# A two-layer RWKV-7 / linear-attention / cross-attention trunk on one core: decay ahead of the attention heads, output gates ahead of the norm, a second query buffer, six early gates instead of four

## The chip, the cores and the metric

The kernel runs on one core of a Trainium2 chip, as one launch. The metric is the device time of that launch in microseconds, the median of several runs. TensorE (PE) does the matrix products, VectorE (DVE), ScalarE (ACT) and GpSimd (POOL) the elementwise work, and the queue of SyncE (SP) issues the DMAs. SBUF holds the working tiles, PSUM the results of products.

## The reference

Two layers, each on 512 tokens of 1024 channels (all float32):

```python
for l in range(DEPTH):                                   # DEPTH = 2
    x = x + 0.5 * swiglu_ffn(rmsnorm(x, ffn1_norm[l]), ffn1_w_in[l], ffn1_w_out[l])
    h = rmsnorm(x, mix_norm[l])
    u_rwkv, u_gla, u_xa, u_gate = split_cols(h @ w_in[l], ...)
    y_rwkv, v_first = rwkv7_mixer(u_rwkv, v_first, ...)  # 8 heads of 64, a recurrence over the tokens
    y_gla = gla_mixer(u_gla, ...)                        # 4 heads, chunks of 64, decay, RMS norm, SiLU gate
    y_xa = memory_attention(u_xa, rmsnorm(mem, mem_norm[l]), xa_w_kv[l])   # 4 heads, 256 memory rows
    gates = sigmoid(u_gate)                              # one per branch and channel
    merged = sum over the branches j of (branch_j @ w_branch[l, j]) * gates[j]
    x = x + merged @ w_out[l]
    x = x + 0.5 * swiglu_ffn(rmsnorm(x, ffn2_norm[l]), ffn2_w_in[l], ffn2_w_out[l])
return rmsnorm(x, final_norm)
```

In the linear attention (GLA) a pair of heads needs q, k and v (projections, a short causal convolution, SiLU), a decay E = exp(gcum) and F = exp(-gcum) from a projection `al`, masked products inside chunks, a recurrence over 8 chunks, and at the end `o * rsqrt(mean(o*o)) * norm_w * silu(go)`; `go` is the output gate.

## The kernel before

Everything is kept with channels on the partitions and the 512 tokens along the free axis. A large product is made of 128x128 weight blocks. Weights come from HBM as `wraw`; ACT copies them to a rounded part `whi`, DVE subtracts to get the rest `wlo` (L581 to L598), activations are split in the same way (`xhi` and `xlo`, `yh` and `yl`, `mhi` and `mlo`), and each block costs three matmuls (`mm3`, L608): hi times hi, hi times lo, lo times hi, all into one PSUM tile `ps_b` of 512 columns. There are three `ps_b` buffers. One projection of the normed input h (`proj`, L717) is 8 blocks, so 24 such matmuls; one product with a branch weight is 12. The text calls these matmuls large. The small ones are those of GLA, of the attention heads and of RWKV (`ps_i`, `ps_f`, `ps_c`, `ps_y`).

A layer is FFN1, the mixing stage (`mix`, L1271) and FFN2. The mixing stage computes the keys and values of the memory (`xa_proj`), the norm (`norm_mix`, L634), then the projection `al`, the attention heads 0 and 1, GLA pair 0, the shared parts of RWKV (`rwkv_lora`: six projections), GLA pair 1, and then RWKV in eight half steps (`rwkv_fill`, L1043). After each half step a share of a list of fillers is called: heads 2 and 3, and the gated outputs of GLA and of attention (`branch`, L1260: one gate projection of 24 large matmuls, one product of 12). The two projections that the next pair of RWKV heads needs (`rwkv_rkv`, L748) stand between these in the program. Last come four early gates for RWKV's own output (`gate`, L1254), RWKV's last output and the `w_out` product.

No order of instructions is written by hand. A recorder (class at L248) takes the program down as operations with dependencies, plans the order with a cost for each operation (`cost`, `run`, `plan`, L311 to L478), and issues it; each engine then works through its own order. On PE an operation of kind 0 (the small matmuls) goes before those of kind 1 (the large ones of `mm3`), and within a kind the program's order counts (L379). So the large matmuls run in the order of the program and are put wherever no small one is ready. A tile waits for the release of the tile `bufs` places ahead of it in the ring of its tag, so a large product waits until the `ps_b` three ahead of it has been read, and a large product that can't be read out holds up all large products behind it. A tile of a pool that opens waits until the pools closed before have been left by all their users (`Pool`, L193).

What the change and the prediction touch: `gla_pair` (L1165) calls `gla_conv` for q and k, then `gla_decay`; `gk` is the tile of k and then of each v, `gc` the scratch tile of the convolution and of the norm, each with one buffer; the gate projection `GGO` stands inside the norm at the pair's end, and SiLU of it is written to `gc2`. `xa_query` (L1091) puts a head's query into `xq`, which has one buffer, is overwritten with the head's result and is stored to `yx` by a DMA. `sumsq` and `rstd` (L646, L658) make the sum of squares `sqa` and the factor `rs` of a norm in the pool `nrm`, which stays open.

Of the kernel before, what the change touches and what calls it, by code (L numbers as in the profile page):

```python
# [11 lines left out]
F32 = mybir.dt.float32  # L12
# [7 lines left out]
P = 128  # L20
T = 512
# [473 lines left out]
class Net:  # L495
# [128 lines left out]

    def norm_in(self, name):
# [5 lines left out]
        rs, _ = self.rstd(self.x, T, D)  # L631
        return [(hi[:, k, :], lo[:, k, :]) for k in range(KD)], rs

    def norm_mix(self):  # L634
# [4 lines left out]
        rs, _ = self.rstd(self.x, T, D, copy=False)  # L639
# [6 lines left out]
    def sumsq(self, xs, n):  # L646
        nc = self.nc
        acc = self.nrm.tile([P, n], F32, name="sqa", tag="sqa")
        for k, x in enumerate(xs):
            if k == 0:  # L650
                nc.scalar.activation(acc, x, AF.Square)
                continue
            sq = self.nrm.tile([P, n], F32, name="sq", tag="sq", bufs=2)
            nc.scalar.activation(sq, x, AF.Square)
            nc.vector.tensor_tensor(acc, acc, sq, ALU.add)
        return acc

    def rstd(self, xs, n, dim, copy=True):  # L658
        nc = self.nc
        acc = self.sumsq(xs, n)  # L660
        nt = n // P
        ps = self.small()
        for t in range(nt):
            nc.tensor.matmul(ps[:, t:t + 1], acc[:, t * P:(t + 1) * P], self.c("ones")[:, 0:1], start=True, stop=True)
        rt = self.nrm.tile([P, nt], F32, name="rt", tag="rt", bufs=2)
        nc.scalar.activation(rt, ps[:, 0:nt], AF.Sqrt, bias=self.eps[:, 0:1], scale=1.0 / dim)
        nc.vector.reciprocal(rt, rt)
        ps = self.small()
        for t in range(nt):
            nc.tensor.matmul(ps[:, t * P:(t + 1) * P], rt[:, t:t + 1].to_broadcast([P, P]), self.c("ident"),  # L670
                             start=True, stop=True)
        if not copy:
# [135 lines left out]
    def rwkv_first(self, hp, hf, r, k, v, kk, kh, a, G):  # L808
# [85 lines left out]
        nc.vector.tensor_tensor(z4[:, :, 3:4], z4[:, :, 3:4], t4[:, :, 0:1], ALU.add)  # L894
        KH = rw.tile([P, 4, P], F32, name="KH", tag="KH", bufs=1)
        for c in range(4):
            nc.scalar.activation(KH[:, c, :], KBc[:, c, :], AF.Copy, scale=E[:, c, 64:65])

        ps = self.small("i")
        for c in range(4):  # L900
            nc.tensor.transpose(ps[:, c * P:(c + 1) * P], KH[:, c, :], self.c("ident"))
        KBT = rw.tile([P, 4, P], F32, name="KBT", tag="KBT", bufs=2)
# [188 lines left out]
    def xa_query(self, pool, j):  # L1091
        ps = self.proj(XQ + j)
        q = pool.tile([P, T], F32, name="xq", tag="xq", bufs=1)
        self.nc.scalar.activation(q, ps, AF.Copy)
        return q

    def xa_head(self, pool, j, q, kT, vm):
        nc = self.nc
        sc = 128.0 ** -0.5
        for hh in range(2):  # L1100
# [19 lines left out]
            pt = pool.tile([P, 2, 256], F32, name="pt", tag="pt", bufs=1)  # L1120
            nc.scalar.activation(pt, ps.rearrange("p (m t) -> p m t", m=2), AF.Copy)
# [42 lines left out]

    def gla_pair(self, pool, hp, al, yh, yl):  # L1165
        nc = self.nc
        t = lambda name, bufs=1: pool.tile([P, T], F32, name=name, tag=name, bufs=bufs)
        q, k = t("gq"), t("gk")
        self.gla_conv(pool, hp, q)
        self.gla_conv(pool, 2 + hp, k)  # L1170
        E, F = self.gla_decay(pool, hp, al)
        qz = self.qz
# [49 lines left out]
        for n in range(7):  # L1222
            src = kv[n % 2][:, (n // 2) * P:(n // 2 + 1) * P]
            if n == 0:
                nc.vector.tensor_copy(St[:, 0, :], src)
            else:
                nc.vector.scalar_tensor_tensor(St[:, n, :], St[:, n - 1, :], Ec[:, n, 63:64], src, ALU.mult, ALU.add)
        for j in range(2):
            h = 2 * hp + j
# [9 lines left out]
            nc.scalar.activation(o, ps, AF.Copy)  # L1239
            sq = t("gc")  # L1240
# [3 lines left out]
            sd = t("gc")  # L1244
# [26 lines left out]
    def mix(self):  # L1271
        nc, I, l = self.nc, self.I, self.l
        with ExitStack() as octx:
# [8 lines left out]
            kT, vm = self.xa_proj(self.keep, *ybuf())  # L1282
            self.h = self.norm_mix()

# [11 lines left out]
            with ExitStack() as ctx:  # L1296
# [6 lines left out]
                with ExitStack() as c2:  # L1303
# [31 lines left out]
            for m in range(KD):  # L1335
                self.branch(0, m, yh, yl, False, gates[m] if m < 4 else None)
                self.split(mhi[:, m, :], mlo[:, m, :], self.x[m], 0.5)
# [9 lines left out]
    def mem_norm(self):  # L1347

        nc, I = self.nc, self.I
        with ExitStack() as ctx:  # L1350
            pool = self.pool("memp", 1, ctx)
            mt = [pool.tile([P, NMEM], F32, name=f"m{k}", tag=f"m{k}") for k in range(KD)]
            for k in range(KD):
                nc.sync.dma_start(out=mt[k], in_=I["mem"][k * P:(k + 1) * P, :])
            rs, rt = self.rstd(mt, NMEM, D, copy=False)
            self.rsm = self.const.tile([P, NMEM], F32, name="rsm", tag="rsm")
# [4 lines left out]
    def finish(self, out):  # L1361
        nc = self.nc
        rs, _ = self.rstd(self.x, T, D, copy=False)
# [80 lines left out]
```

## Time and profile before

| | |
|---|---|
| median of 3 runs | 2858.64 us (2857.74 to 2858.75) |
| profiled execution | 2867.46 us |
| its span | 2865.7 us |
| mean granted TensorE clock | 0.976 |
| PE matmul busy | 2775.7 us (97%) |
| DVE, ACT busy | 1575.8 us (55%), 1167.4 us (41%) |
| DMA | 258.04 MB, mean 90 GB/s |

In the views below PE is the matmul engine and PEld the loading of its weights, which overlaps it. Matmuls are pipelined: one that starts every 0.227 us is shown with a length of 0.39 us, and so "busy" is the time in which at least one was under way. A bracket at the end of a row gives the idle time of that engine just before, and what ended it. PEclk is the share of the full TensorE clock that was granted. Tile names lose their buffer numbers. Nearly all instructions carry one line, L278, that of the recorder, so the reading goes by the tiles' names.

### The profile page before, as it was taken

Reading aid. Unit: us, or ns where it says so; the run is one execution under the profiler, and the core shown is the slowest. Engines: PE = TensorE matmul, PEld = TensorE weight load, DVE = VectorE, ACT = ScalarE, POOL = GpSimd, SP = SyncE. Lnnn points to the kernel's source line nnn. Section 1 sums busy time; section 2 is a strip of 40 time slices with the busy share of each in tenths; the row PEclk is TensorE's granted clock in tenths of the full one; section 3 lists DMA queues with packets and bytes.
Section 4 is the critical chain, followed back from the end, with each engine's and each line's share of the span. In section 5 each row is a group of like instructions: output and inputs, shape, how many; then the busy total and the mean of one; then the engine's idle time right before and its main releaser. Section 6 shows DMA issues by size and latency. Waiting matters only on the chain.

```text
span 2865.7 us, 35465 instructions
## 1 busy us (share of the span) xinstructions
PE 2775.7 (97%) x13280; PEld 2257.5 (79%) x13280; DVE 1575.8 (55%) x3056; ACT 1167.4 (41%) x2150; POOL 19.8 (1%) x102
## 2 busy tenths in 40 slices
PE   8999998998999899999999999989989998999998
PEld 6888887786788688888888888867777876888886
DVE  6434454675767655444554444655766685544443
ACT  5323345454445343323433233554544453432332
POOL 0000000000000000000000000000000000000000
PEclk9999997999999899999999999979999998999999
DMA  5232331211221132222322223312112211322222
GB/s 187 87 105 96 112 125 59 96 61 45 71 88 58 55 121 96 90 101 93 108 102 95 101 95 125 120 41 92 58 56 90 70 57 57 122 98 91 101 94 83
DMA packets 91723, 258.04 MB, mean 90 GB/s; under 512 B 10464, under 2 KB 24832, under 8 KB 91552
## 3 DMA queue, kind: packets, MB, share of 16 engines
q1 hardware_dynamic: 91552, 255.79, 25.8%
q8 instruction: 104, 1.70, 0.2%
q14 instruction: 67, 0.55, 0.1%
HBM read 243.69 MB, written 12.06 MB: 89 GB/s over the span
## 4 chain that ended last, share of the span: by engine, by line
PE 92%; DVE 5%; ACT 2%; issue 1%; DMA 1%; DVEq 0%; ACTq 0%; SPq 0%
PE ps_b L278 78%; PE ps_i L278 4%; PE ps_f L278 4%; PE ps_c L278 3%; PE ps_y L278 2%; DVE y L278 1%; DVE wlo L278 1%; ACT whi L278 0%; DMA x<-in_x_dram 0%; DVE Z L278 0%; ACT L278 0%; DVE st L278 0%; ACT VU L278 0%; DVE tt L278 0%; DVE t L278 0%
## 5 line engine op out<-in xcount | busy, mean ns | idle before, releaser
L278 ACT ACTIVATE whi<-wraw 128x512 fp32r<-128x512 f32 (+1 forms) x874 | 544.3, 623 | 1208.6 <-PE ps_b L278 1170.9
L278 PE MATMUL ps_b<-xhi,whi 128*128 128x512 f32 x2288 | 911.8, 399 | 16.3 <-ACT whi L278 9.7
L278 PE MATMUL ps_b<-xlo,whi 128*128 128x512 f32 x2288 | 906.7, 396 | 0.3 <-DVE xlo L278 0.3
L278 PE MATMUL ps_b<-xhi,wlo 128*128 128x512 f32 x2288 | 905.5, 396 | 1.1 <-DVE wlo L278 1.0
L278 DVE TENSOR_TENSOR wlo<-wraw,whi 128x512 fp32r<-128x512 f32 (+1 forms) x874 | 590.7, 677 | 573.9 <-ACT whi L278 572.4
L278 PEld LDWEIGHTS ps_b<-xhi,whi 128*128 128x128 f32 x2288 | 431.5, 189 | 112.0 <-ACT whi L278 11.6
L278 PEld LDWEIGHTS ps_b<-xhi,wlo 128*128 128x128 f32 x2288 | 430.9, 188 | 93.6 <-DVE wlo L278 3.9
L278 PEld LDWEIGHTS ps_b<-xlo,whi 128*128 128x128 f32 x2288 | 430.9, 188 | 92.9 <-issue 3.6
L278 PE MATMUL ps_b<-mhi,whi 128*128 128x512 f32 x704 | 277.4, 394 | 0.0
L278 PE MATMUL ps_b<-mhi,wlo 128*128 128x512 f32 x704 | 276.0, 392 | 0.0
L278 PE MATMUL ps_b<-mlo,whi 128*128 128x512 f32 x704 | 273.2, 388 | 0.0
L278 PEld LDWEIGHTS ps_b<-mhi,wlo 128*128 128x128 f32 x704 | 132.1, 188 | 31.0
L278 PEld LDWEIGHTS ps_b<-mlo,whi 128*128 128x128 f32 x704 | 132.2, 188 | 29.6
L278 PEld LDWEIGHTS ps_b<-mhi,whi 128*128 128x128 f32 x704 | 132.3, 188 | 26.3
L278 DVE TENSOR_TENSOR fm<-ps_b,ft 128x512 f32<-128x512 f32 x88 | 60.9, 692 | 127.7 <-PE ps_b L278 127.6
L278 DVE TENSOR_TENSOR ft<-ps_b,rs 128x512 f32<-128x512 f32 x88 | 60.9, 692 | 122.7 <-PE ps_b L278 122.5
L278 PE MATMUL ps_b<-yh,whi 128*128 128x512 f32 (+1 forms) x256 | 96.8, 381 | 4.6 <-ACT yh L278 4.6
L278 ACT ACT_TABLE_LOAD x73 | 93.7, 1283 | 17.6 <-DVE mx L278 7.7
L278 PE MATMUL ps_b<-yl,whi 128*128 128x512 f32 (+1 forms) x256 | 98.2, 384 | 0.0
L278 PE MATMUL ps_b<-yh,wlo 128*128 128x512 f32 (+1 forms) x256 | 97.1, 379 | 0.0
L278 DVE SCALAR_TENSOR_TENSOR x<-ps_b,x 128x512 f32<-128x512 f32 x64 | 44.3, 692 | 61.1 <-PE ps_b L278 61.0
L278 DVE TENSOR_TENSOR ft<-ft,rs 128x512 f32<-128x512 f32 x88 | 61.0, 693 | 13.5 <-ACT ft L278 5.4
(261 smaller groups left out, 2811.4 us busy)
## 6 DMA issues: line engine op xcount, KB each, us to landing
wraw<-in_ffn_in_dram SPq DMA_DIRECT2D x176, 512.0 KB, 3.4
wraw<-in_w_main_dram SPq DMA_DIRECT2D x108, 512.0 KB, 3.5
wraw<-in_ffn_out_dram SPq DMA_DIRECT2D x64, 512.0 KB, 3.5
wraw<-in_ffn_out_dram SPq DMA_DIRECT2D x64, 192.0 KB, 2.3
wraw<-in_w_branch_dram SPq DMA_DIRECT2D x48, 256.0 KB, 2.5
wraw<-in_w_out_dram SPq DMA_DIRECT2D x16, 512.0 KB, 3.4
xd<-x SPq DMA_DIRECT2D x16, 256.0 KB, 2.2
wraw<-in_w_k_dram SPq DMA_DIRECT2D x8, 512.0 KB, 3.6
```

The source lines that it names most:

```text
L278: return getattr(getattr(self.tc.nc, engine), what)(*(f(v) for v in a), **{n: f(v) for n, v in k.items()})
```

## The change

1. The decay of a GLA pair is computed first. `gla_pair` calls `gla_decay`, then a function `between` that it is given, then the convolutions of q and k. For pair 0 `between` is the attention heads 0 and 1, which stood ahead of the pair; for pair 1 it is `rwkv_lora`.
2. The two output gates of a pair (projection and SiLU) are computed ahead of the pair's norm loop, into the tile `gs` of the pool `mx`, instead of inside it into `gc2`.
3. `xq` gets two buffers, `gk` two, `gc` two (and `gc2` goes: the reciprocal is written in place). `pt` of a head takes the buffer of `pr`.
4. Head 3 stands after four outputs of GLA in the list of fillers, not after two.
5. Six early gates are made, not four; two new tiles `eg0` and `eg1` hold the added ones.
6. Space for this: `sqa` and `rs` of a norm are taken from the FFN's pool (or, in `mix`, from a pool `nm` that is open during `norm_mix` alone) instead of `nrm`; RWKV's tile `KH` goes, its values are written over `KB`.

```diff
-        acc = self.nrm.tile([P, n], F32, name="sqa", tag="sqa")
+        acc = pool.tile([P, n], F32, name="sqa", tag="sqa", bufs=1)
...
-        rs = self.nrm.tile([P, n], F32, name="rs", tag="rs", bufs=1)
+        rs = pool.tile([P, n], F32, name="rs", tag="rs", bufs=1)
...
             pool = self.pool("ffn", 2, ctx)
-            xs, rs = self.norm_in(norm)
+            xs, rs = self.norm_in(norm, pool)
...
-        KH = rw.tile([P, 4, P], F32, name="KH", tag="KH", bufs=1)
         for c in range(4):
-            nc.scalar.activation(KH[:, c, :], KBc[:, c, :], AF.Copy, scale=E[:, c, 64:65])
+            nc.scalar.activation(KBc[:, c, :], KBc[:, c, :], AF.Copy, scale=E[:, c, 64:65])
...
-        q = pool.tile([P, T], F32, name="xq", tag="xq", bufs=1)
+        q = pool.tile([P, T], F32, name="xq", tag="xq", bufs=2)
...
-        a = pool.tile([P, T], F32, name="gc", tag="gc", bufs=1)
+        a = pool.tile([P, T], F32, name="gc", tag="gc", bufs=2)
...
-    def gla_pair(self, pool, hp, al, yh, yl):
+    def gla_pair(self, pool, hp, al, yh, yl, between):
         nc = self.nc
         t = lambda name, bufs=1: pool.tile([P, T], F32, name=name, tag=name, bufs=bufs)
-        q, k = t("gq"), t("gk")
+        E, F = self.gla_decay(pool, hp, al)
+        between()
+        q, k = t("gq"), t("gk", 2)
         self.gla_conv(pool, hp, q)
         self.gla_conv(pool, 2 + hp, k)
-        E, F = self.gla_decay(pool, hp, al)
...
-            v = t("gk")
+            v = t("gk", 2)
...
+        gate = []
+        for j in range(2):
+            s = self.mx.tile([P, T], F32, name="gs", tag="gs", bufs=2)
+            nc.scalar.activation(s, self.proj(GGO + 2 * hp + j), AF.Silu)
+            gate.append(s)
         for j in range(2):
...
-            ri = t("gc2")
+            ri = sd
             nc.vector.reciprocal(ri, sd)
             nc.vector.scalar_tensor_tensor(o, o, self.pcol("gla_norm", h), ri, ALU.mult, ALU.mult)
-            s = t("gc2")
-            nc.scalar.activation(s, self.proj(GGO + h), AF.Silu)
-            nc.vector.tensor_tensor(o, o, s, ALU.mult)
+            nc.vector.tensor_tensor(o, o, gate[j], ALU.mult)
...
-            self.h = self.norm_mix()
+            with ExitStack() as ctx:
+                self.h = self.norm_mix(self.pool("nm", 1, ctx))
...
-                    head(0)
-                    head(1)
-                    self.gla_pair(gp, 0, al, yh, yl)
-                    self.rwkv_lora()
-                    self.gla_pair(gp, 1, al, yh, yl)
+                    self.gla_pair(gp, 0, al, yh, yl, lambda: (head(0), head(1)))
+                    self.gla_pair(gp, 1, al, yh, yl, self.rwkv_lora)
...
-                fill = [part(head, 2)] + [part(self.branch, 1, m, yh, yl, True) for m in range(2)] + [part(head, 3)]
-                fill += [part(self.branch, 1, m, yh, yl, True) for m in range(2, KD)]
+                fill = [part(head, 2)] + [part(self.branch, 1, m, yh, yl, True) for m in range(4)] + [part(head, 3)]
+                fill += [part(self.branch, 1, m, yh, yl, True) for m in range(4, KD)]
...
-                gates = [self.gate(0, m, eg[m // 2][:, (m % 2) * T:(m % 2 + 1) * T]) for m in range(4)]
+                eg = [e[:, i * T:(i + 1) * T] for e in eg for i in range(2)]
+                eg += [self.mx.tile([P, T], F32, name="early", tag=f"eg{i}", bufs=1) for i in range(2)]
+                gates = [self.gate(0, m, g) for m, g in enumerate(eg)]
```

The program has as many PE instructions as before and as many loads of ACT's tables (73); the planner puts them in another order. Three places on PE matter here.

The first is GLA pair 0, in layer 0. In the order before, these rows of PE stand where the keys of the pair are first transposed (`ps_i<-cst,gq`, then the first v, `gk`) and multiplied (`qz`, `kg`, `qr`, `kr`):

```order
L278 MATMUL ps_b<-xhi,whi 128x512
L278 MATMUL ps_b<-xlo,whi 128x512
L278 MATMUL ps_b<-xhi,wlo 128x512
L278 MATMUL ps_i<-cst,gq 128x128 x4
L278 MATMUL ps_i<-cst,gk 128x128 x4
L278 MATMUL ps_i<-qz_2887,kg 128x128
L278 MATMUL ps_i<-qr,kr 128x128
```

And of the change, at the same transposes:

```order
L278 MATMUL ps_b<-xhi,whi 128x512
L278 MATMUL ps_b<-xlo,whi 128x512
L278 MATMUL ps_i<-cst,gq 128x128 x4
L278 MATMUL ps_b<-xhi,wlo 128x512
L278 MATMUL ps_b<-xhi,whi 128x512
L278 MATMUL ps_b<-xlo,whi 128x512
L278 MATMUL ps_b<-xhi,wlo 128x512
L278 MATMUL ps_i<-qz_3021,kg 128x128
L278 MATMUL ps_i<-qr,kr 128x128
```

The transposes moved 70 rows up, and large matmuls now stand behind them. The product that the decay starts from (`ps_f<-al,aup`) stands 31 large matmuls ahead of these transposes before and 120 in the change.

The second place is where attention head 2 ends and head 3 begins (`kT,xq` are a head's scores, `pr` the transposes of its softmax, `pt,vm` its result; each twice in a head). Before, with the second half of head 2 and the first scores of head 3:

```order
L278 MATMUL ps_f<-cst,pr 128x128 x4
L278 MATMUL ps_f<-pt,vm 128x256 x2
L278 MATMUL ps_f<-kT,xq 128x256 x2
L278 MATMUL ps_f<-cst,pr 128x128 x4
L278 MATMUL ps_f<-pt,vm 128x256 x2
L278 MATMUL ps_f<-kT,xq 128x256 x2
L278 MATMUL ps_b<-xhi,whi 128x512
```

In the change, head 2 at its first softmax:

```order
L278 MATMUL ps_f<-cst,pr 128x128 x4
L278 MATMUL ps_b<-yh,wlo 128x512
L278 MATMUL ps_b<-xhi,whi 128x512
L278 MATMUL ps_b<-xlo,whi 128x512
L278 MATMUL ps_b<-xhi,wlo 128x512
L278 MATMUL ps_b<-xhi,whi 128x512
L278 MATMUL ps_f<-pt,vm 128x256 x2
L278 MATMUL ps_b<-xlo,whi 128x512
L278 MATMUL ps_b<-xhi,wlo 128x512
L278 MATMUL ps_b<-xhi,whi 128x512
L278 MATMUL ps_b<-xlo,whi 128x512
L278 MATMUL ps_f<-kT,xq 128x256 x2
```

Six groups of small matmuls stood behind one another with no large one between; now large ones of the gated outputs stand between all of them, and head 3 comes some 130 rows later.

The third place is the end of RWKV's recurrence in layer 0 (`ps_y<-S,AR`, `ps_f<-qs,Z` and `ps_f<-VU,KBT` are the steps of the chain, `ps_y<-VU,GR` its output, `ps_f<-cst,y` the transposes after the output's norm). Before:

```order
L278 MATMUL ps_f<-qs_85,Z 128x128
L278 MATMUL ps_f<-VU,KBT 128x128
L278 MATMUL ps_y<-S_89,AR 128x128
L278 MATMUL ps_f<-qs_91,Z 128x128
L278 MATMUL ps_y<-VU,GR 128x128 x4
L278 MATMUL ps_f<-cst,y 128x128 x2
L278 MATMUL ps_f<-sgl,g_221 128x256
L278 MATMUL ps_b<-yh,whi 128x512 x3
```

In the change:

```order
L278 MATMUL ps_f<-VU,KBT 128x128
L278 MATMUL ps_b<-xhi,whi 128x512
L278 MATMUL ps_b<-xlo,whi 128x512
L278 MATMUL ps_b<-xhi,wlo 128x512
L278 MATMUL ps_b<-yh,whi 128x512
L278 MATMUL ps_y<-S_89,AR 128x128
L278 MATMUL ps_b<-yl,whi 128x512
L278 MATMUL ps_b<-yh,wlo 128x512
L278 MATMUL ps_b<-yh,whi 128x512
L278 MATMUL ps_b<-yl,whi 128x512
L278 MATMUL ps_b<-yh,wlo 128x512
L278 MATMUL ps_f<-qs_91,Z 128x128
```

The last steps of the chain had no large matmul between them; now three to five stand between these, and 20 between `ps_y<-VU,GR` and `ps_f<-cst,y`. Behind `ps_f<-sgl,g` both orders read alike: large matmuls that need RWKV's last output.

More of the change, by code (lines that the diff above doesn't have):

```diff
@@ L623, in split, with norm_in @@
             nc.vector.scalar_tensor_tensor(lo, src, scale, hi.bitcast(F32), ALU.mult, ALU.subtract)
-    def norm_in(self, name):
+    def norm_in(self, name, pool):
         hi = self.keep.tile([P, KD, T], F32R, name="xhi", tag="xhi")
@@ L630, in norm_in, with norm_mix @@
             self.split(hi[:, k, :], lo[:, k, :], self.x[k], self.pcol(name, k))
-        rs, _ = self.rstd(self.x, T, D)
+        rs, _ = self.rstd(self.x, T, D, pool)
         return [(hi[:, k, :], lo[:, k, :]) for k in range(KD)], rs
-    def norm_mix(self):
+    def norm_mix(self, pool):
         nc = self.nc
@@ L638, in norm_mix @@
         lo = self.keep.tile([P, KD, T], F32R, name="xlo", tag="xlo")
-        rs, _ = self.rstd(self.x, T, D, copy=False)
+        rs, _ = self.rstd(self.x, T, D, pool, copy=False)
         for k in range(KD):
@@ L644, in norm_mix, with sumsq @@
         return [(hi[:, k, :], lo[:, k, :]) for k in range(KD)]
-    def sumsq(self, xs, n):
+    def sumsq(self, xs, n, pool):
         nc = self.nc
-        acc = self.nrm.tile([P, n], F32, name="sqa", tag="sqa")
+        acc = pool.tile([P, n], F32, name="sqa", tag="sqa", bufs=1)
         for k, x in enumerate(xs):
@@ L656, in sumsq, with rstd @@
         return acc
-    def rstd(self, xs, n, dim, copy=True):
+    def rstd(self, xs, n, dim, pool, copy=True):
         nc = self.nc
-        acc = self.sumsq(xs, n)
+        acc = self.sumsq(xs, n, pool)
         nt = n // P
@@ L894, in rwkv_first @@
         nc.vector.tensor_tensor(z4[:, :, 3:4], z4[:, :, 3:4], t4[:, :, 0:1], ALU.add)
[L895 removed]
         for c in range(4):
[L897 removed]
+            nc.scalar.activation(KBc[:, c, :], KBc[:, c, :], AF.Copy, scale=E[:, c, 64:65])
         ps = self.small("i")
         for c in range(4):
[L901 removed]
+            nc.tensor.transpose(ps[:, c * P:(c + 1) * P], KBc[:, c, :], self.c("ident"))
         KBT = rw.tile([P, 4, P], F32, name="KBT", tag="KBT", bufs=2)
@@ L1119, in xa_head @@
                     nc.tensor.transpose(ps[:, o:o + P], pr[:, t, m * P:(m + 1) * P], self.c("ident"))
-            pt = pool.tile([P, 2, 256], F32, name="pt", tag="pt", bufs=1)
+            pt = pool.tile([P, 2, 256], F32, name="pt", tag="pr", bufs=1)
             nc.scalar.activation(pt, ps.rearrange("p (m t) -> p m t", m=2), AF.Copy)
@@ L1239, in gla_pair @@
             nc.scalar.activation(o, ps, AF.Copy)
-            sq = t("gc")
+            sq = t("gc", 2)
             nc.scalar.activation(sq, o, AF.Square)
@@ L1335, in mix @@
             for m in range(KD):
-                self.branch(0, m, yh, yl, False, gates[m] if m < 4 else None)
+                self.branch(0, m, yh, yl, False, gates[m] if m < len(gates) else None)
                 self.split(mhi[:, m, :], mlo[:, m, :], self.x[m], 0.5)
@@ L1354, in mem_norm @@
                 nc.sync.dma_start(out=mt[k], in_=I["mem"][k * P:(k + 1) * P, :])
-            rs, rt = self.rstd(mt, NMEM, D, copy=False)
+            rs, rt = self.rstd(mt, NMEM, D, pool, copy=False)
             self.rsm = self.const.tile([P, NMEM], F32, name="rsm", tag="rsm")
@@ L1362, in finish @@
         nc = self.nc
-        rs, _ = self.rstd(self.x, T, D, copy=False)
+        rs, _ = self.rstd(self.x, T, D, self.nrm, copy=False)
         for k in range(KD):
```

2 lines of the change are left out of this document (1 added, 1 removed).

## The prediction

> **What bounds the kernel now.** I read the page first, then the idle time and the granted clock of PE stretch by stretch, then the rows that end the long waits. The page:
>
> ```profile
> span 2865.7 us, 35465 instructions
> PE 2775.7 (97%) x13280; PEld 2257.5 (79%) x13280; DVE 1575.8 (55%) x3056; ACT 1167.4 (41%) x2150; POOL 19.8 (1%) x102
> ```
>
> PE is busy in 97% of the span, so the number of matmuls bounds the kernel, and the change leaves that number alone. It can only touch the 90 us in which PE is idle, and the time that PE is busy at half its clock. Both sit in few places. The next view gives, for stretches that I cut at them, the length, then the busy time of PE (and the number of matmuls) and of the others; the third value from the right is PEclk, the granted clock.
>
> ```profile
> 30.00:376.00 346.00, 346.00 (x1524) 285.50 (x1523) 160.30 (x248) 117.11 (x190) 0.00 (x0) 1.00 0.30 104
> 460.50:466.80 6.30, 0.00 (x0) 0.00 (x0) 4.56 (x7) 4.82 (x6) 0.00 (x0) 0.75 0.20 73
> 466.80:494.80 28.00, 27.99 (x129) 23.05 (x130) 11.32 (x24) 8.70 (x13) 0.00 (x0) 0.51 0.00 1
> 494.80:515.00 20.20, 15.49 (x63) 11.18 (x62) 13.82 (x15) 16.03 (x22) 0.00 (x0) 1.00 0.15 54
> 655.00:685.50 30.50, 21.12 (x73) 14.71 (x72) 11.81 (x37) 9.90 (x26) 0.20 (x1) 0.78 0.07 22
> 685.50:957.00 271.50, 269.16 (x1544) 217.60 (x1542) 196.34 (x526) 129.44 (x307) 4.43 (x21) 1.00 0.21 70
> 957.00:985.80 28.80, 17.23 (x65) 12.51 (x65) 11.70 (x37) 6.63 (x18) 0.00 (x0) 0.70 0.05 17
> 1873.50:1879.80 6.30, 0.01 (x1) 0.01 (x1) 4.56 (x7) 4.82 (x6) 0.00 (x0) 0.75 0.19 74
> 1879.80:1908.00 28.20, 28.20 (x129) 23.26 (x129) 11.54 (x24) 8.69 (x12) 0.00 (x0) 0.50 0.00 1
> 1908.00:1930.00 22.00, 17.29 (x63) 11.92 (x62) 13.90 (x16) 16.32 (x22) 0.00 (x0) 0.94 0.16 57
> 2013.20:2016.70 3.50, 1.98 (x8) 0.69 (x6) 2.27 (x5) 3.09 (x4) 0.12 (x1) 0.99 0.39 145
> 2016.70:2020.10 3.40, 3.40 (x8) 2.72 (x9) 1.33 (x2) 1.25 (x2) 0.00 (x0) 0.50 0.01 5
> 2086.00:2105.40 19.40, 12.90 (x45) 9.32 (x44) 5.77 (x15) 6.87 (x19) 0.00 (x0) 0.74 0.04 14
> 2380.00:2409.00 29.00, 17.47 (x65) 12.96 (x66) 11.86 (x38) 6.63 (x18) 0.00 (x0) 0.71 0.02 8
> ```
>
> The first row is FFN1: no idle time, full clock, 346.00 / 1524 = 0.227 us for a large matmul; this is the price of filler. Then come three places per layer: GLA pair 0 (460 to 515, and 1873 to 1930), heads 2 and 3 inside RWKV (655 to 685, 2086 to 2105), the end of RWKV (957 to 985, 2380 to 2409). Between them, 685 to 957, PE is busy in 269.16 of 271.50 us. What ended the waits stands in brackets in the order of time:
>
> ```profile
> 466.81 1.12 PE L278 MATMUL ps_i<-cst,gq 128*128 128x128 f32 x4 [6.37 <-DVE gq L278]
> ...
> 679.08 0.60 ACT L278 ACTIVATE xq<-ps_b 128x512 f32<-128x512 f32 x1 [2.10 <-DMA yx<-xq]
> ...
> 679.73 2.07 PE L278 MATMUL ps_f<-kT,xq 128*128 128x256 f32 x4 [3.17 <-ACT xq L278]
> ...
> 977.43 0.66 PE L278 MATMUL ps_f<-cst,y 128*128 128x128 f32 x2 [5.77 <-DVE y L278]
> ...
> 981.25 1.22 PE L278 MATMUL ps_b<-yh,whi 128*128 128x512 f32 x2 [2.30 <-ACT yh L278]
> ```
>
> In each case the filler had run out. At 460 the gate projections of the pair hold two of the three `ps_b`, because their SiLU goes to a tile that the unfinished norm needs, and nothing large can start. At 677 head 3's query can't be written until head 2's result has left `xq` by DMA. At the end of RWKV the four early gates are used up, and three unfinished outputs, which need RWKV's last quarter, hold the three `ps_b`.
>
> **GLA pair 0.** The wait of 6.37 us is for the chain that begins with the decay:
>
> ```profile
> 453.21 0.69 ACT L278 ACTIVATE gz<-ps_f,par 128x512 f32<-128x512 f32 x1 [1.59 <-PE ps_f L278]
> ...
> 466.07 0.69 DVE L278 TENSOR_TENSOR gq<-kg,gE 128x512 f32<-128x512 f32 x1
> ```
>
> From `gz` to the end of `gq` it takes 13.6 us. Before, 31 large matmuls stand between the product that starts it and the transposes of `gq`: 31 x 0.227 = 7.0 us of cover. In the change there are 120, or 27 us, so the decay is no longer late. What is last there is then k's own convolution, with 29 large matmuls (6.6 us) and the small ones of head 1 behind k's product. I take the wait of 6.3 us in each layer as gone.
>
> The clock goes with it. After the wait the clock stays at 0.51 for 28.00 us though PE is busy in 27.99 of them. The same small matmuls in pair 1 at full clock give the price; first pair 0, then pair 1 (count, busy time, mean):
>
> ```profile
> L278 PE MATMUL ps_y<-qz,St 128*128 128x64 f32 x28 | 6.6, 373 | 0.0
> ```
>
> ```profile
> L278 PE MATMUL ps_y<-qz,St 128*128 128x64 f32 x28 | 4.3, 264 | 0.1
> ```
>
> By this ratio 28.0 us shrink by 28.0 x (1 - 4.3 / 6.6) = 9.8 us; if everything halves, by 14. I take 12 in layer 0, and 13 in layer 1, where the 22.00 us behind it ran at 0.94 (0.06 x 22 = 1.3).
>
> The Trainium skill, page "TensorE: Matmul & The Clock Gate", section "What's actually happening", says that one busy window of about 3.4 us brings the full clock back. The two rows at 466.80 and 1879.80 speak against it for small matmuls. By the rule a dip would be worth about 1.7 us, the two terms of 12 and 13 would shrink to that, and the total below would be an estimated 57 in place of 78, so 2802.
>
> The 4.7 us of idle time behind (20.20 - 15.49, 22.00 - 17.29) are waits for read-outs of `ps_b` behind the norm's reciprocals on DVE, with two buffers held by the gates. With SiLU of the gates ahead of the norm they are free; I take them as gone.
>
> What comes in place: the transposes of the second v. From the end of its product, its convolution runs through these steps (ACT scales, DVE adds three taps, with two masks `pf` of the products between, ACT's SiLU):
>
> ```profile
> 468.46 0.68 ACT L278 ACTIVATE gc<-ps_b,par 128x512 f32<-128x512 f32 x1
> ...
> 466.19 0.63 ACT L278 ACTIVATE gk<-gc 128x512 f32<-128x512 f32 x1 [1.40 <-DVE kr L278]
> ...
> 561.80 2.31 DVE L278 SCALAR_TENSOR_TENSOR gc<-ps_b,par,gc 128x511 f32<-128x511 f32 x3
> ...
> 554.84 0.75 DVE L278 TENSOR_TENSOR pf<-ps_i,cst 128x256 f32<-128x256 f32 x2
> ```
>
> 0.68 + 2.31 + 0.75 + 0.63 = 4.4 us, about 5.4 with the hand-overs. In the change's order PE has five large matmuls (1.1 us) and some twelve small ones (about 2) meanwhile, so 2.5 us stay open, and 1.5 more where the chunk recurrence `St` is built: 4 us of new waits, between 0 (the large matmuls of the first gate are ready and may have been placed well) and 7. Sum: 6.3 + 12 + 4.7 - 4 = 19 in layer 0, 20 in layer 1.
>
> **Heads 2 and 3.** Idle time: 30.50 - 21.12 = 9.4 us and 19.40 - 12.90 = 6.5. The two buffers remove the wait for the DMA, and with head 3 behind four outputs of GLA there are large matmuls between all small groups of head 2 (second place of the order). I leave 1.5 and 1 us idle. The clock: 0.22 x 30.5 = 6.7 us if PE were busy throughout the slow part, 6.7 - 9.4 / 2 = 2.0 if all idle time lay in it; I take 3.5, and 2.5 in layer 1 (5.0 and 1.8 by the same steps). Sum: 11.4 and 8. The projections of the next RWKV heads stand behind these fillers in the program, so the recurrence goes on earlier by the same time.
>
> **The end of RWKV.** Idle time: 28.80 - 17.23 = 11.6 us, 29.00 - 17.47 = 11.5. Two more gates are 48 x 0.227 = 10.9 us of filler, taken out of the stretch behind, where PE is the bound. They don't fit wholly: the last wait of 2.30 us has the same rows around it as before, and of the 5.77 us the 20 large matmuls now placed there cover 4.5, so 3.5 us stay idle and 8 go; the other 2.9 us of filler stretch the chain. The clock: 0.30 x 28.8 = 8.6 at most, 8.6 - 11.6 / 2 = 2.8 at least; 3 go, since the 3.5 us that stay idle may still cost a short dip. Sum: 11 in each layer.
>
> **What the space costs.** `sqa` in the FFN's pool waits for the pools before it to be left, so the sum of squares starts only after the last matmul of the stage before. In `mix` the norm's factor then reaches PE after 97 of the memory's 144 large matmuls, not after 37, and the norm's work falls on a DVE that is full:
>
> ```profile
> 383.00:401.00 18.00, 18.00 (x108) 15.86 (x107) 17.73 (x32) 11.90 (x21) 0.00 (x0) 1.00 0.42 146
> ```
>
> 24 of these 32 steps still lie behind the factor, 24 x 17.73 / 32 = 13.3 us, against 47 + 21 large matmuls (15.4 us) until `al` needs the last of them. That nearly fits; 1 us per layer, between 0 and 3. At the FFN starts the factor comes after 45 or 46 large matmuls (43 and 21 before), at the first one after 62 (40 before); it is needed when the fourth product wants a `ps_b`, after 72. Nothing there. `KH` over `KB`, `pt` over `pr`, the reciprocal in place: each waits for readers that are done first; nothing. Without that cover the cost would be a fraction of a microsecond in each of 16 half steps.
>
> **Sum.** 19 + 20 + 11.4 + 8 + 11 + 11 - 2 = 78.4 us. The profiled execution took 2867.46 us, 8.8 more than the median of 2858.64; 78.4 us from it is 2789.1, and from the median 2780.
>
> **Rivals.** (A) *The clock falls in the new GLA block all the same.* The rows at 2013.20 and 2016.70 show the price of short waits: 1.98 us busy of 3.50, and the next 3.4 us at 0.50. Two to four microseconds of waits among few large matmuls can do this, and the small ones behind stay slow until large ones follow, which in the change is soon (13 and 24 in a row after the pair). About half the old dip, 6 us a layer: 2780 + 12 = 2792; if it begins early, all 25: 2805. For it: this block has the fewest large matmuls. Against it: pair 1, ordered likewise, has no such dip. 35%. The Trainium skill, page "TensorE: Matmul & The Clock Gate", section "A second HAM failure mode: psum-queue depth-cycling", says that short idle times between groups of matmuls make the clock swing; the row at 2013.20 agrees.
>
> (B) *The fillers are given back.* If RWKV's chain and not PE limits 685 to 957, the gain at heads 2 and 3 (19.4 us) returns as idle time at RWKV's end: 2780 + 19.4 = 2799. Against it: 269.16 of 271.50 us busy. 12%.
>
> (C) *The norm's factor comes too late* (slower). Five norms now start after the last matmul of the stage before, and the first of all comes later too. If the factor came after more than 72 large matmuls, all three `ps_b` would stand full and PE would wait. To turn the sum it would have to cost over 13 us at each of six starts, that is to come 70 or more large matmuls later than it stands: 2865. 3%.
>
> (D) *The order is made for the planner's costs, and on the chip the added large matmuls stand in the way of the chain* as much as they fill: no change, 2859. 2%.
>
> **How the numbers follow.** My forecast, 2780, has 48%; its own bounds (new waits 0 to 7 us a layer, clock 9.8 to 14, heads' and end's clock, the norm) reach from 2762 to 2796. The range goes up to take in A and B: 2762 to 2808. A measurement of this kernel can tell about 0.2%, 6 us, from no change; beyond that faster has 0.95, within it 0.02, slower 0.03.
>
> **What would show it.** Right: no wait over 3 us before `ps_i<-cst,gq`, PEclk near 1.00 through GLA pair 0, no `xq` waiting for a DMA, the wait before `ps_f<-cst,y` at about 1.3 us and the one before `ps_b<-yh,whi` still 2.3. Wrong: PEclk at 0.5 for 10 us or more in GLA pair 0 (A), more idle time at RWKV's end than 4 us (B), waits of `ps_b` products for `rs` or `xlo` (C).

## The result, and the profile after

| | before | after |
|---|---|---|
| median | 2858.69 us (2857.74 to 2861.76, 4 runs) | 2769.98 us (2768.55 to 2770.58, 4 runs) |
| profiled execution, its span | 2867.46 us, 2865.7 us | 2769.8 us, 2768.0 us |
| mean granted TensorE clock | 0.976 | 0.995 |
| PE busy | 2775.7 us | 2731.8 us |
| span less PE busy | 90.0 us | 36.2 us |

The change makes the kernel 88.7 us faster, a ratio of 0.9687 (95% interval 0.967 to 0.9704). 2780 with a range of 2762 to 2808 was forecast.

The page of after:

```profile
span 2768.0 us, 35481 instructions
PE 2731.8 (99%) x13280; PEld 2225.2 (80%) x13280; DVE 1570.7 (57%) x3056; ACT 1164.9 (42%) x2150; POOL 19.8 (1%) x102
```

The same 13280 matmuls, 43.9 us less busy time on PE (the clock) and 53.8 us less idle time: 97.7 us between the two profiled executions. The view by stretches has the places of before again, in the same columns (length, busy time of PE, PEld, DVE, ACT and POOL, then PEclk; the last two are the DMA's busy share and its GB/s):

```profile
383.00:401.00 18.00, 18.00 (x96) 13.96 (x96) 15.63 (x28) 12.03 (x22) 0.28 (x6) 1.00 0.43 150
436.00:467.00 31.00, 30.85 (x196) 24.40 (x195) 19.97 (x41) 19.87 (x31) 0.00 (x0) 1.00 0.16 57
467.00:525.00 58.00, 57.78 (x254) 47.16 (x252) 36.19 (x49) 33.61 (x50) 0.20 (x2) 1.00 0.35 123
640.00:700.00 60.00, 59.34 (x356) 47.69 (x356) 46.37 (x128) 33.05 (x84) 0.93 (x5) 1.00 0.18 58
934.00:947.10 13.10, 9.24 (x30) 6.87 (x29) 7.18 (x22) 3.50 (x6) 0.00 (x0) 0.74 0.07 21
1806.00:1833.00 27.00, 26.85 (x179) 21.09 (x178) 17.42 (x38) 16.67 (x26) 0.00 (x0) 1.00 0.13 44
1833.00:1890.00 57.00, 57.00 (x238) 43.08 (x237) 31.48 (x41) 31.84 (x48) 0.20 (x2) 1.00 0.35 119
2000.00:2060.00 60.00, 58.76 (x324) 47.10 (x324) 45.81 (x130) 33.68 (x79) 1.13 (x6) 1.00 0.22 72
2311.50:2322.70 11.20, 7.69 (x24) 5.56 (x23) 6.21 (x19) 3.08 (x5) 0.00 (x0) 0.70 0.00 0
```

The first row is the memory's keys beside the norm (no idle time). The second and third are GLA pair 0 of layer 0 with the end of its norm, the sixth and seventh the same in layer 1: 0.37 us idle (0.15 + 0.22) and 0.15 us where 11.0 stood (6.3 + 4.7), at full clock. Heads 2 and 3 (fourth and eighth) have 0.7 and 1.2 us idle in 60, none of it before a head's matmuls. At the end of RWKV 3.9 and 3.5 us are left, in the waits that the forecast left there (timeline of PE, layer 0, then layer 1):

```profile
938.11 0.41 PE L278 MATMUL ps_f<-cst,y 128*128 128x128 f32 x2 [1.21 <-DVE y L278]
...
941.61 1.65 PE L278 MATMUL ps_b<-yh,whi 128*128 128x512 f32 x3 [2.65 <-ACT yh L278]
...
2314.24 0.41 PE L278 MATMUL ps_f<-cst,y 128*128 128x128 f32 x2 [1.20 <-DVE y L278]
...
2317.38 1.65 PE L278 MATMUL ps_b<-yh,whi 128*128 128x512 f32 x3 [2.30 <-ACT yh L278]
```

The one place of pair 0 where the forecast put new waits is the second v. Its product ends at about 447.9 us, its transposes stand last in these rows of PE:

```profile
447.75 1.03 PE L278 MATMUL ps_f<-pt,vm 128*128 128x256 f32 x4
448.71 0.49 PE L278 MATMUL ps_i<-qz,kg 64*128 64x128 f32 x2
...
450.40 0.48 PE L278 MATMUL ps_b<-xhi,whi 128*128 128x512 f32 x1
...
451.51 0.48 PE L278 MATMUL ps_i<-qz,kg 64*128 64x128 f32 x2
...
452.59 0.50 PE L278 MATMUL ps_b<-xlo,whi 128*128 128x512 f32 x1
452.93 0.60 PE L278 MATMUL ps_i<-cst,gk 128*128 128x128 f32 x4
```

No row has a bracket, and those left out have none either: PE waited nowhere in these 5.0 us.

### The profile page after: what moved, and what is told of

Its sections match the earlier page's. It is cut to its first block, busy times and chain, and to the rows that moved or that the text cites. A ratio compares the mean times of both kernels' runs of the same rounds, so it can differ in the third digit from the quotient of the medians.

```text
span 2768.0 us, 35481 instructions
## 1 busy us (share of the span) xinstructions
PE 2731.8 (99%) x13280; PEld 2225.2 (80%) x13280; DVE 1570.7 (57%) x3056; ACT 1164.9 (42%) x2150; POOL 19.8 (1%) x102
## 5 line engine op out<-in xcount | busy, mean ns | idle before, releaser
L278 PEld LDWEIGHTS ps_b<-mlo,whi 128*128 128x128 f32 x704 | 132.1, 188 | 29.6
L278 DVE TENSOR_TENSOR ft<-ft,rs 128x512 f32<-128x512 f32 x88 | 60.9, 693 | 14.1 <-ACT ft L278 6.3
```

Of the source, the lines that this page charges most:

```text
L278: return getattr(getattr(self.tc.nc, engine), what)(*(f(v) for v in a), **{n: f(v) for n, v in k.items()})
```

## The experiments

Twelve kernels. Eleven start from the changed kernel (2769.98 us) and one from the kernel before. The kernel before ran beside them at medians of 2860.4 (first four below), 2855.6 (next four) and 2857.5 us (last four).

| kernel | median us | ratio to before (95%) | against after |
|---|---|---|---|
| decay late | 2769.88 | 0.9685 (0.9666 to 0.9704) | -0.1 |
| gates late | 2771.97 | 0.9692 (0.9673 to 0.9711) | +2.0 |
| both late | 2799.61 | 0.9789 (0.9769 to 0.9808) | +29.6 |
| decay late, one gk | 2769.46 | 0.9683 (0.966 to 0.9705) | -0.5 |
| four early gates | 2793.30 | 0.9769 (0.9752 to 0.9785) | +23.3 |
| heads as before | 2792.26 | 0.9770 (0.9751 to 0.9789) | +22.3 |
| GLA pair as before | 2792.83 | 0.9767 (0.9745 to 0.9789) | +22.9 |
| eight early gates | 2756.72 | 0.9644 (0.9629 to 0.9659) | -13.3 |
| GLA pair as before, one xq | 2808.60 | 0.9827 (0.9809 to 0.9845) | +38.6 |
| one xq | 2773.01 | 0.9700 (0.9684 to 0.9715) | +3.0 |
| head 3 early | 2769.97 | 0.9689 (0.9674 to 0.9705) | 0.0 |
| space alone, on before | 2856.09 | 0.9995 (0.9986 to 1.0005) | |

**Decay late.**

```diff
-        E, F = self.gla_decay(pool, hp, al)
-        between()
         q, k = t("gq"), t("gk", 2)
         self.gla_conv(pool, hp, q)
         self.gla_conv(pool, 2 + hp, k)
+        E, F = self.gla_decay(pool, hp, al)
...
-                    self.gla_pair(gp, 0, al, yh, yl, lambda: (head(0), head(1)))
-                    self.gla_pair(gp, 1, al, yh, yl, self.rwkv_lora)
+                    head(0)
+                    head(1)
+                    self.gla_pair(gp, 0, al, yh, yl)
+                    self.rwkv_lora()
+                    self.gla_pair(gp, 1, al, yh, yl)
```

> The changed kernel with item 1 alone undone: the decay stands behind the convolutions of q and k again, heads 0 and 1 ahead of pair 0, the shared parts of RWKV ahead of pair 1. Gates ahead of the norm and second buffers stay. In the order about 65 large matmuls now stand between the decay's product and the transposes of gq (31 before, 120 in the change): 65 x 0.227 = 14.8 us against a chain of 13.6 us. Theory 1 (the wait is a matter of the large matmuls that can start, and the clock falls only after a wait): wait of 0 to 1.5 us, no dip, 2770 to 2776. Theory 2 (the decay's place is the cause, whatever the gates do): the wait of 6.3 us and the dip come back, 19 + 20 us less the 9.4 us of later waits, about 2800.

2769.88 us: nothing comes back. The stretch of its pair 0, at full clock with 0.8 us idle:

```profile
445.00:490.00 45.00, 44.20 (x247) 34.59 (x248) 29.94 (x49) 31.61 (x43) 0.05 (x1) 1.00 0.23 75
```

The same with one `gk` (`v = t("gk")`, `k = t("gk")`) is no slower either:

> Item 1 undone, and gk with one buffer again; gates ahead of the norm stay. About 68 large matmuls between the decay's product and the transposes. Theory 1 (cover counts, and either the early gates or the second gk gives it): 2770 to 2778. Theory 3 (the second gk alone gives the cover, since it lets the first v be read out): the wait and the dip come back, about 2800.

2769.46 us. So the decay's place alone is worth nothing while the gates stand ahead of the norm and `xq` has two buffers, and theory 3 falls.

**Gates late.**

```diff
-        gate = []
-        for j in range(2):
-            s = self.mx.tile([P, T], F32, name="gs", tag="gs", bufs=2)
-            nc.scalar.activation(s, self.proj(GGO + 2 * hp + j), AF.Silu)
-            gate.append(s)
...
-            ri = sd
+            ri = t("gc2")
...
-            nc.vector.tensor_tensor(o, o, gate[j], ALU.mult)
+            s = t("gc2")
+            nc.scalar.activation(s, self.proj(GGO + h), AF.Silu)
+            nc.vector.tensor_tensor(o, o, s, ALU.mult)
```

(and one `gc`.)

> The changed kernel with item 2 alone undone: the output gates are made inside the norm again, SiLU goes to gc2, and gc has one buffer. Decay first stays. Forecast's step (the gates hold two ps_b behind the norm's reciprocals): 4.7 us of waits a layer come back, 2779, and up to 8 us more if the clock dips behind them. Rival (those waits were a consequence of the late decay only): no change, 2770.

2771.97 us, 2 slower. The waits of 4.7 us don't come back; the stretch of pair 0 has 0.9 us idle:

```profile
436.00:490.00 54.00, 53.12 (x290) 41.71 (x289) 37.14 (x60) 38.86 (x57) 0.00 (x0) 1.00 0.22 73
```

**Both late** (the two diffs above together).

> Items 1 and 2 undone together; gk keeps its second buffer, heads and early gates stay as changed. Some 60 large matmuls stand between the decay's product and the transposes of gq. Theory 1 (cover counts): the wait of 6.3 us stays away or is under 2 us, 4.7 us a layer of later waits come back, 2775 to 2785. Theory 2 (the decay's place is the cause): the whole term of 19 + 20 us comes back, 2809.

2799.61 us, between the theories. The wait of 6.4 us before the transposes of `gq` stays away, as theory 1 said, but the large matmuls that fill this place are missing behind (timeline of PE; `wlal` and `wlo` are made by DVE, the one for the shared parts of RWKV, the other as the rest of a weight; `gc` here belongs to the pair's norm):

```profile
484.40 0.70 PE L278 MATMUL ps_b<-xhi,whi 128*128 128x512 f32 x1 [4.34 <-DVE wlal L278]
...
492.22 1.12 PE L278 MATMUL ps_i<-gc,cst 128*128 128x512 f32 x2 [1.16 <-ACT gc L278]
494.74 0.50 PE L278 MATMUL ps_b<-xhi,whi 128*128 128x512 f32 x1 [0.70 <-ACT whi L278]
...
498.15 0.80 PE L278 MATMUL ps_b<-xhi,wlo 128*128 128x512 f32 x1 [2.68 <-DVE wlo L278]
```

That is 8.9 us of idle time, where the kernel before had 11.0 in two pieces, and the clock dips for a short time (0.87 in this stretch):

```profile
476.00:502.00 26.00, 17.12 (x65) 12.32 (x64) 15.58 (x15) 20.66 (x26) 0.10 (x1) 0.87 0.09 31
```

The two parts of the change are two ways to the same thing: large matmuls that can start while the pair's chains run. With two `xq`, one is enough; without either, PE waits, early or late.

**GLA pair as before** (both diffs, one `gk`; heads and six gates as changed), and **the same with one xq** (`tag="xq", bufs=1`).

> Everything in the GLA pair as before: decay behind the convolutions, gates inside the norm, one gk, one gc with gc2. Heads and six gates stay as changed. It is the run with both parts undone (2799.6 measured) with the second gk taken away too. Theory 1 (the parts cover for one another, and the second gk is the last cover left): the wait of 6.3 us before ps_i<-cst,gq and the long half clock behind it come back in both layers; what the whole block is worth is then the measured gain of 88.7 less the forecast's terms for heads and end of RWKV, 88.7 - 19.4 - 22 = 47: 2817. By the forecast's own term, 19 + 20: 2809. Theory 2 (the second gk does nothing): 2800.

> The run with the whole GLA pair as before (2792.8 measured, waits of 0.9 + 0.9 us where 6.4 stood), with xq taken back to one buffer as well. In its order 31 large matmuls stand between the decay's product and the transposes of gq, as before; with two xq there were 52. Theory 1 (the second xq, by letting head 1's products run earlier, leaves 21 more large matmuls for pair 0): the wait of 6.4 us and the 28 us at half clock come back in both layers: 2 x (6.4 - 2.6 + 12 - 1.7) = 28 us more than that run, about 2820. Rival (some other part keeps the wait away): 2793 to 2797.

The first took 2792.83 us, less than with two `gk`, and not the 2817 of theory 1. Its four executions are far apart (2786.1 to 2796.2 us), but all lie below the four with two `gk` (2798.1 to 2800.3); why the second `gk` costs time when decay and gates are late, 6.8 us by the medians, wasn't settled. Its waits at the transposes of pair 0:

```profile
459.31 0.66 PE L278 MATMUL ps_i<-cst,gq 128*128 128x128 f32 x4 [0.93 <-DVE gq L278]
460.81 0.66 PE L278 MATMUL ps_i<-cst,gk 128*128 128x128 f32 x4 [0.85 <-ACT gk L278]
```

The second took 2808.60 us, and the wait of before is there to the hundredth, in both layers:

```profile
464.06 1.11 PE L278 MATMUL ps_i<-cst,gq 128*128 128x128 f32 x4 [6.37 <-DVE gq L278]
...
493.34 0.50 PE L278 MATMUL ps_b<-xhi,whi 128*128 128x512 f32 x1 [1.99 <-DVE wlal L278]
...
507.15 0.50 PE L278 MATMUL ps_b<-xhi,whi 128*128 128x512 f32 x1 [2.19 <-DVE v L278]
```

So the second query buffer, which the forecast costed at heads 2 and 3 alone, was a third cover of pair 0: with it head 1's products run earlier, and 52 large matmuls are left for the decay's chain instead of 31. It cost 15.8 us more by the medians (12.4 to 22.5, by which of the four executions above one compares with), and not 28. Between the two profiled executions the idle time rose by 7.1 us, where 7.6 were expected, and the busy time of PE by 9.5, where 20.6 were expected: the difference lies in the clock, below.

**Four early gates.**

```diff
-                eg += [self.mx.tile([P, T], F32, name="early", tag=f"eg{i}", bufs=1) for i in range(2)]
```

> The changed kernel with item 5 alone undone: four early gates. Forecast's term for the end of RWKV: 11 us a layer come back (8 of idle time, 3 of clock): 2792. Rival (the recurrence now ends earlier and other fillers lie beside it, so the last two gates matter less): under 4 us a layer, 2770 to 2778.

2793.30 us, 23.3 slower; 22 was forecast, 16 of them idle time and 6 clock. Against the profile of the changed kernel PE is idle for 16.9 us more and busy for 6.1 us more. The old rows are back:

```profile
940.35 0.66 PE L278 MATMUL ps_f<-cst,y 128*128 128x128 f32 x2 [5.77 <-DVE y L278]
...
944.16 1.65 PE L278 MATMUL ps_b<-yh,whi 128*128 128x512 f32 x3 [2.30 <-ACT yh L278]
```

**Eight early gates**, the last two in the buffers `gs` that the outputs of attention have left.

```diff
+                eg += [self.mx.tile([P, T], F32, name="gs", tag="gs", bufs=2) for i in range(2)]
                 gates = [self.gate(0, m, g) for m, g in enumerate(eg)]
```

> The changed kernel with eight early gates; the last two use the two buffers gs of the pool mx, so no space is added. 48 more large matmuls (10.9 us) are moved ahead of RWKV's last output; in the order 28 of them instead of 20 stand before the transposes ps_f<-cst,y, and the rest behind the product of sgl and g. Theory 1 (those two waits are a lack of large matmuls that can start): the waits of 1.2 and 2.3 us go in both layers, and the 6.8 us of half clock behind them with them: 2 x (3.5 + 2 to 3.4) = 11 to 14 us faster, 2756 to 2759. If the clock dips all the same: 2763. Rival (the chain that ends RWKV is on the path, and more large matmuls only stretch it): 2770 or above.

2756.72 us: theory 1. This version beats both kernels; it needs no space. The ends of RWKV, layer 0 and layer 1, without idle time and at full clock:

```profile
925.00:960.00 35.00, 35.00 (x163) 27.94 (x162) 23.38 (x52) 14.28 (x29) 0.00 (x0) 1.00 0.31 91
2295.00:2330.00 35.00, 35.00 (x162) 28.20 (x163) 23.81 (x53) 14.59 (x29) 0.00 (x0) 1.00 0.28 84
```

The medians differ by 13.3 us, the two profiled executions by 11.8. The idle time fell by 6.8 us (the two places held 3.9 + 3.5), and the busy time of PE by 5.1 us, from 2731.8 us, with the half clock that followed there:

```profile
PE 2726.7 (99%) x13280; PEld 2221.9 (81%) x13280; DVE 1569.7 (57%) x3056; ACT 1164.2 (42%) x2150; POOL 19.8 (1%) x102
```

**Heads as before, one xq, head 3 early.** The first run has both edits.

```diff
-        q = pool.tile([P, T], F32, name="xq", tag="xq", bufs=2)
+        q = pool.tile([P, T], F32, name="xq", tag="xq", bufs=1)
...
-                fill = [part(head, 2)] + [part(self.branch, 1, m, yh, yl, True) for m in range(4)] + [part(head, 3)]
-                fill += [part(self.branch, 1, m, yh, yl, True) for m in range(4, KD)]
+                fill = [part(head, 2)] + [part(self.branch, 1, m, yh, yl, True) for m in range(2)] + [part(head, 3)]
+                fill += [part(self.branch, 1, m, yh, yl, True) for m in range(2, KD)]
```

> The changed kernel with the heads as before: xq has one buffer (item 3 in part) and head 3 stands after two outputs of GLA (item 4). Forecast's term: 11.4 + 8 us come back as waits before ps_f<-kT,xq and as clock: 2789. Rival B of the prediction (what is won there is given back at the end of RWKV): 2770 to 2775.

> The changed kernel with one xq again, head 3 still behind four outputs of GLA. With both of these as before 2792.3 was measured. Theory 1 (head 3's place sets how many large matmuls lie between the heads' steps): 2770 to 2774, no wait before ps_f<-kT,xq. Theory 2 (the buffer and its DMA are the cause, as the forecast said of the wait of 3.17 us): 2778 to 2786.

> The changed kernel with head 3 behind two outputs of GLA again, xq with two buffers. Theory 1 (head 3's place is what matters): 2785 to 2792. Theory 2 (the buffer is what matters): 2770 to 2776. If each alone is enough, as with the two parts in GLA, both this run and the one with one xq lie at 2770 to 2776.

Both edits undone gave 2792.26 us, 22.3 slower: by the profiles 13.0 us of idle time (13.4 forecast) and 7.9 of busy time (6 forecast). One undone gave 2773.01 (one `xq`) and 2769.97 (head 3 early). Again each edit alone is enough, or nearly, which was the third case of the last expectation. In the first run the old waits are back, in layer 0:

```profile
644.87 0.72 PE L278 MATMUL ps_f<-cst,pr 128*128 128x128 f32 x4 [2.09 <-DVE pr L278]
646.28 1.13 PE L278 MATMUL ps_f<-pt,vm 128*128 128x256 f32 x4 [0.69 <-ACT pt L278]
650.58 1.33 PE L278 MATMUL ps_f<-kT,xq 128*128 128x256 f32 x4 [3.17 <-ACT xq L278]
```

The stretches from 630 and from 2000 us, with heads 2 and 3 in them, have 8.2 and 8.9 us idle in the first run

```profile
630.00:700.00 70.00, 61.84 (x328) 48.70 (x326) 43.78 (x115) 33.64 (x82) 1.02 (x5) 0.98 0.16 50
2000.00:2080.00 80.00, 71.07 (x374) 55.78 (x375) 50.49 (x139) 35.48 (x90) 1.74 (x8) 0.94 0.18 57
```

and in that with head 3 early (two xq)

```profile
630.00:700.00 70.00, 68.36 (x374) 55.19 (x373) 47.06 (x126) 37.78 (x93) 1.03 (x5) 1.00 0.19 63
2000.00:2080.00 80.00, 78.83 (x444) 63.18 (x442) 58.50 (x164) 43.61 (x109) 1.13 (x6) 1.00 0.22 71
```

only 1.6 and 1.2. The ends of RWKV wait as long in all three as in the changed kernel, so nothing was given back there: rival B falls.

**Space alone**, on the kernel before: `sqa` and `rs` in the pool of their stage, `KH` over `KB`.

```diff
-        acc = self.nrm.tile([P, n], F32, name="sqa", tag="sqa")
+        acc = pool.tile([P, n], F32, name="sqa", tag="sqa", bufs=1)
...
-        rs = self.nrm.tile([P, n], F32, name="rs", tag="rs", bufs=1)
+        rs = pool.tile([P, n], F32, name="rs", tag="rs", bufs=1)
...
-            nc.scalar.activation(KH[:, c, :], KBc[:, c, :], AF.Copy, scale=E[:, c, 64:65])
+            nc.scalar.activation(KBc[:, c, :], KBc[:, c, :], AF.Copy, scale=E[:, c, 64:65])
```

> The kernel before with item 6 alone: sqa and rs in the FFN's pool or in nm, KH over KB; nothing else. Forecast's term: 2 us slower (0 to 6), against before at 2855 to 2861. Rival C (the norm's factor comes too late): 13 us and more at a start, over 2870. Rival (it does nothing): 0.

2856.09 us, no difference. The later norm costs nothing, and rival C falls.

**The clock behind one and the same wait.** The wait of 6.37 us stands in three profiled executions, twice in each, before the same small matmuls. The half clock behind it lasted 28.00 and 28.20 us in that of the kernel before. In that of the kernel with the space alone it is these stretches, in layer 0 with the stretch that follows:

```profile
465.60:475.80 10.20, 8.84 (x37) 7.43 (x38) 5.63 (x12) 3.00 (x6) 0.00 (x0) 0.50 0.00 0
475.80:490.00 14.20, 13.62 (x106) 11.16 (x107) 7.01 (x15) 7.49 (x10) 0.00 (x0) 1.00 0.01 2
1868.50:1889.00 20.50, 16.94 (x91) 14.66 (x91) 12.46 (x28) 5.04 (x8) 0.00 (x0) 0.50 0.00 1
```

And in that with the GLA pair as before and one `xq`:

```profile
459.90:480.40 20.50, 16.34 (x88) 14.15 (x89) 12.29 (x27) 5.61 (x9) 0.00 (x0) 0.50 0.00 0
...
1849.10:1859.30 10.20, 8.41 (x36) 7.25 (x36) 6.07 (x12) 2.92 (x5) 0.00 (x0) 0.50 0.00 0
```

In these four places the half clock lasts 10.2 or 20.5 us, the wait's tail included. In the kernel before, counted in the same way, half clock stands from 463.6 to 494.3 us and from 1876.7 to 1910.8 us, so 30.7 and 34.1 (the two rows of 28 us begin only where the wait ends, and the second stops short): the execution that the forecast priced had the longest dips of the three. That is most likely the 8.8 us by which it lay above its median. The execution with the space alone was 11.5 us shorter with 92.0 us of idle time against 90.0; all of the difference is busy time of PE, 2762.2 against 2775.7 us. The 13 runs of the kernel before beside the last four kernels lie between 2853.1 and 2864.1 us, while the changed kernel's four lie within 2.0 us. (The wait of 6.37 us is not the only source of such a spread: the kernel with the GLA pair as before and two `xq`, without this wait, spread by 10.1 us in four executions.) The Trainium skill, page "TensorE: Matmul & The Clock Gate", section "What's actually happening", says that the window by which the clock is granted runs free and that the same kernel's slow start therefore varies from run to run; dips of 10.2 to 34.1 us behind one wait agree with that. Its rule that one busy window of about 3.4 us is enough agrees with none of the six: even the last of these rows has PE busy for 8.41 us at half clock.

## Why the prediction was right, point by point

- **What bounds the kernel.** Right. The number of matmuls stayed and the time came out of idle time and clock: 53.8 and 43.9 us. So rival D, no change, falls.
- **GLA pair 0, the mechanism.** Half right. The wait and the dip went, as forecast, and their removal is worth 38.6 us by the run that brings them back; 19 + 20 were forecast. That these agree is luck: the two profiled executions differ by 22.5 us of idle time and 14.1 of busy time of PE (clock), and the forecast had 14 (22 less the new waits of 8, which didn't come) and 25 (from the longest dips). But the forecast credited the decay's place with 6.3 + 12 us and the gates' with 4.7 a layer. The runs show that these are not terms of a sum: with the second `xq` and either of the two, all but 0 to 2 us of the 38.6 are there, and the second `xq` by itself gives 15.8 of them by the medians. Whether one of the two is enough with a single `xq` wasn't run. The forecast had named the common cause (the filler had run out) and then costed each cure against its own wait.
- **The new waits, 4 us a layer.** Wrong, and the largest miss in idle time: 0.37 and 0.15 us idle in the whole pair, the low end of 0 to 7. The chain of the second v was sized well (5.4 us, measured 5.0 from the end of its product to its transposes). What failed is the count on PE: "some twelve small ones" with five large. From the first of the rows above to the last stand 26 small ones (4 of head 1's result, 16 of the keys' products, 4 and 2 of the recurrence and the output), and they fill the time. 22 of them are the pair's own, so the forecast undercounted these; the 4 of head 1, which moved behind the decay and now lies inside the pair, are the smaller part of the miss. Where the recurrence is built, 1.5 us were forecast and no wait stands.
- **Rival A.** The waits that should have dropped the clock weren't there. Its mechanism exists: in the run with both parts late, the idle time from 480 us on goes with a clock of 0.87, and the run loses 29.6 us for 2 x 9 us of waits. That the small matmuls stay slow until large ones follow is not borne out: with the space alone the clock came back at 475.8 us, among small ones, 10.2 us after it had fallen; the only two large ones in between, at 473 us, stand in the kernel before too, where the clock stayed at half until 494.3 us.
- **Heads 2 and 3.** 19.4 forecast, 22.3 measured by undoing both edits. The leftovers of 1.5 and 1 us aren't there. The forecast gave the gain to both edits together, which was right, and the wait for the DMA to the buffer; but either edit removes PE's wait.
- **The end of RWKV.** Right in the rows: 1.21 and 2.65, 1.20 and 2.30 us left of 1.3 and 2.3; 23.3 measured, 22 forecast.
- **Space.** -2 forecast, nothing measured (0.9986 to 1.0005); the stretch beside the norm has no idle time in the changed kernel (18.00 of 18.00 us).
- **The sum.** Between the two profiled executions the forecast's 78.4 us lacks 19.3: 10.4 of idle time (new waits 8, the leftovers at the heads most of the rest), 6.9 of clock, 2 of space. Against the median it lacks 10.3, if the 8.8 us of that execution lay in its dips. The clock's term of 37 us is then about 35 by medians (30.4 between the execution with the space alone and the changed kernel). The term that was mis-sized most, against the execution that it was priced from, is the new waits.
- **What stays open.** Undoing by parts gives 38.6 (GLA pair and one `xq`) + 19.3 (head 3, given one `xq`: 2792.3 - 2773.0) + 23.3 = 81.2 of the 88.7 us, if these parts add. The other 7.5 were not placed. By the profiles the parts hold 22.5 + 12.8 + 16.9 = 52.2 of the 53.8 us of idle time, so what is missing is busy time of PE, that is clock; the kernel before alone spreads by 11 us over executions.

## What to carry to other kernels

Where several edits cure the same lack (here: large matmuls that can start while a chain runs), don't add their gains: ask for each what is left when the others are made, and test them undone in pairs. Count everything that the engine has in the stretch, the small work of the block itself and of its neighbour too, before pricing a new wait. And where a wait is left beside an empty buffer, try one more step of filler: two more gates, in buffers that lay idle, gave 13.3 us.

## What the runs showed of the hardware

- The length of the half clock behind one wait of 6.37 us differs where the same small matmuls follow: 10.2, 10.2, 20.5, 20.5, 30.7 and 34.1 us in six places of three kernels, which is 3, 3, 6, 6, 9 and 10 times 3.41 us. What in a stretch of small matmuls brings the clock back was not found.
- The same small matmuls run at full clock when no such wait stands ahead of them: 44.20 of 45.00 us busy at 1.00 in the run with the decay late, with large ones among them. And they kept it once it was back: 13.62 of 14.20 us busy at 1.00 from 475.80 us in the run with the space alone, nearly all small ones up to 486.8 us.
